# Scores of the first and last row group as three rounded products

## The chip, the cores and the metric

The kernel runs on one core of a Trainium2 chip. The metric is the device time of one execution in microseconds (us), the median of the runs. Every number of the profile comes from one profiled execution.

## What is computed

One layer of a transformer trunk: x is 2048 tokens (a grid of 32 rows by 64 columns) of 1024 features. After an RMS norm one projection gives queries, keys, values and a gate, for 16 heads of 64 features. Each token attends to the keys in a window of 8 rows by 16 columns around it, with a learned bias per offset and head. The result is gated, projected and added to x, and a last RMS norm follows.

```
h = rmsnorm(x, norm_0)
q, k, v, gate = split(h @ w_in_0, 4)
s = q . k / sqrt(64) + bias[row offset, column offset]   # in the 8 x 16 window, else -1e30
o = softmax(s) . v
x = x + (o * silu(gate)) @ w_out_0
out = rmsnorm(x, norm_f)
```

All inputs and outputs are float32.

## The kernel before

**Two kinds of matmul.** A large product of float32 data is written as three products of rounded operands: each operand t is split into h, t rounded to the type fp32r by ScalarE (ACT), and l = t - h, by VectorE (DVE), and TensorE (PE) sums h.h, h.l and l.h in one PSUM bank. Projections (L435, L559, L379 to L383) and the output product (L1346 to L1350) are of this kind. Scores (L1027) and the product of probabilities and values (L1134) are single float32 matmuls, of which each shows as two matmul records in the trace; the transposes (L1112) are float32 too, of one record each.

**Stages.** Stages one and two compute most of the projections and store queries, keys, values and gates in DRAM. From about 572 us on the main loop runs 33 cycles, m = 0 to 32. A cycle takes one pair (p, T) of `order`: two heads p and a group T of 8 grid rows. First come the eight head pairs with T = 0 (m = 0 to 7), then T = 1 and 2 in turn (m = 8 to 23), then T = 3 (m = 24 to 31). A group has keys of 11, 15, 15 and 12 grid rows (T = 0 to 3).

**A cycle.** The order of all instructions is written out by hand: what Python emits first stands first in the queue of its engine, and each engine works its queue in order. In cycle m the loop (L1429 to L1489)

- issues loads for later cycles through SyncE's queue (`begin`): keys and queries of cycle m + 1, values of m, gates of m - 1;
- feeds PE with some 16.5 matmuls of 512 columns of the remaining projections, later of the output product (`feed`; in the last group 60 and more), and calls `normalise` for the second half of cycle m - 1: a reciprocal on DVE (L1046), scalings by GpSimd (POOL, L1055) and two by ACT (L1053);
- takes a raw weight tile and splits it (`consume`: L189 on ACT, L190 on DVE), or splits rows for the output product (L1198, L1199), and runs the chain of small DVE operations for the final norm (`run_roots`: L1248 to L1255);
- transposes the probabilities of cycle m - 1 (`turns`) into six PSUM banks, which three copies on ACT and three on DVE empty (L1088);
- computes the scores of cycle m (`scores`, twice, each for two blocks of columns and two heads). A head's queries and keys lie on 64 partitions, so the two heads of a pair use the two halves of PE's rows. Every block and head takes a PSUM bank; DVE adds the bias and takes the maximum (L1035), ACT the exponential (L1041);
- multiplies the probabilities of m - 1 with the values (`values`, L1134), and DVE applies the gate (L1140).

There are eight PSUM banks, handed out as they come free. In cycle 0 there is nothing to normalise or to transpose: 8 matmuls are fed, a few more, and then come the scores.

**Buffers the change touches.** Queries and keys come as float32 into `qp` and `kp` (two buffers each), gates into `sp` (two buffers of 512 columns). `lp` (one buffer) is a landing place of the stages ahead of the loop and serves the last head pair at the end. Stages one and two use buffers of these pools, among them both of `sp`, as `slots` for split operands (L580, L805).

Of the kernel before, what the change touches and what calls it, by code (L numbers as in the profile page):

```python
# [10 lines left out]
F32 = mybir.dt.float32  # L11
F32R = mybir.dt.float32r
BF16 = mybir.dt.bfloat16
I32 = mybir.dt.int32
AF = mybir.ActivationFunctionType
OP = mybir.AluOpType
# [4 lines left out]
ROWS, GW, KH, KW = 32, 64, 8, 16  # L21
# [12 lines left out]
KEY_ROWS = [(0, 11), (4, 19), (12, 27), (20, 32)]  # L34
# [36 lines left out]
def build(ctx, tc, x, xr, xt, wg, rpb, last, w_out, n0, nf, masks, out):  # L71
    nc = tc.nc
# [8 lines left out]
    def pool(name, bufs):  # L81
        p = ctx.enter_context(tc.tile_pool(name=name, bufs=bufs))
        return lambda shape, dt, nm: p.tile(shape, dt, name=nm, tag=name)
# [3 lines left out]
    wp = pool("wp", 8)  # L87
    raw = pool("raw", 6)
    kp = pool("kp", 2)
    qp = pool("qp", 2)  # L90
    vp = pool("vp", 2)
    vhalf = []
# [4 lines left out]
            vhalf.extend((t[:, :512], t[:, 512:]))  # L97
        return vhalf.pop(0)

    sp = pool("sp", 2)  # L100
    xp = pool("xp", 8)
    mkp = pool("mkp", 1)
    pt = pool("pt", 1)
    mp = pool("mp", 10)
    ep = pool("ep", 2)

    def sixths():
        t = pt([128, 3072], F32R, "sixths")
        return [t[:, i * 512:i * 512 + 512] for i in range(6)]

    lp = pool("lp", 1)
# [5 lines left out]
    def bank(n, name):  # L117
        return banks.tile([128, n], F32, name=name, tag="bank")
# [138 lines left out]
    for n, (k, j, ph, c) in enumerate(halves):  # L257
        a = (KINDS[k] + j, ph)
# [79 lines left out]
    def must(*keys):  # L338
        assert all(k in written for k in keys), keys
        for n in range(len(later) - 1, -1, -1):  # L340
            if later[n][1] in keys:
                for _ in range(n + 1):
                    later.pop(0)[2]()
                break
# [225 lines left out]
    def stage_one():  # L570
# [6 lines left out]
        land["x12"] = [kp([128, 960], F32, "land")[:, :512] for _ in range(2)] + [xp([128, 512], F32, "land") for _ in range(2)]  # L577
        sixth = sixths()
        land["x21"] = [spot[:, k] for k in range(3)] + [lp([128, 512], F32, "land")]
        slots = [(mp, 512)] * 8 + [(sp, 512)] * 2 + sixth[:2] + [(vh, 512)] * 4  # L580
        slots += sixth[2:] + [(mp, 512)] * 2 + [(qp, 512)] * 2

        def load(f, k):
# [163 lines left out]
        for k in range(4):  # L747
            y = ev([128, 512], F32, "y")
            a, b, c = land["x11"][k], land["x12"][k], land["x22"][k]
# [48 lines left out]
    def stage_two():  # L798
        x12, x11, x21 = L2["x12"], L2["x11"], L2["x21"]
        x22 = [xp([128, 512], F32, "land") for _ in range(4)]  # L800
        sixth = sixths()
        for k in range(4):
            load_x(2, "x22", k, x22[k])
        slots = {"T2": [(mp, 512)] * 8,
                 "T3": [(sp, 512)] * 2 + sixth[:5] + [(lp, 512)],  # L805
                 "T4": [(vh, 512)] * 4 + [(mp, 512)] * 2 + [sixth[5], (qp, 512)]}

        def also(n, i):
# [120 lines left out]


    KT, VT, QT, EM, SG, E = {}, {}, {}, {}, {}, {}
    LAST, stored_at = {}, {}
    order = [(p, 0) for p in range(NP)] + [(p, T) for p in range(NP) for T in (1, 2)] + [(p, 3) for p in range(NP)]
    pairs = [(p, T, (h, h + 1)) for p, T in order for h in (0, 2)]
# [9 lines left out]
    def load_k(p, T):  # L944
        r0, r1 = KEY_ROWS[T]
        n = (r1 - r0) * GW
        must(*[("k", p, c) for c in range(r0 // 8, (r1 + 7) // 8)])

        def keys():
            t = kp([128, 960], F32, "kt")  # L950
            KT[p, T] = t.rearrange("p (r c) -> p r c", c=GW)
            nc.sync.dma_start(t[:, :n], kd[p][:, r0 * GW:r1 * GW])

        return keys

    def load_q(p, T):
        must(("q", p, T))
# [58 lines left out]
    def scores(i, between=None):  # L1016
        p, T, cs = pairs[i]
        kt, qt = KT[p, T], QT[p, T]
        r0, r1 = KEY_ROWS[T]
        got = []  # L1020
        for C in cs:
            c0, c1 = KEY_COLS[C]
            qs = slice(C * 128, C * 128 + 128)
            pst = [bank((r1 - r0) * (c1 - c0), f"s{s}") for s in range(2)]
            for s in range(2):
                a = slice(s * 64, s * 64 + 64)
                nc.tensor.matmul(pst[s], qt[a, qs], kt[a, :r1 - r0, c0:c1].rearrange("p r (s c) -> p s r c", c=8), start=True, stop=True)  # L1027
            got.append((C, pst))
        ST[i] = st = tiny.tile([128, 12], F32, name="st")
        for j, (C, pst) in enumerate(got):  # L1030
            n = (r1 - r0) * width(C)
            X[i, C] = [xp([128, 512], F32, f"x{s}")[:, :n] for s in range(2)]
            for s in range(2):
                o = 2 * j + s
                nc.vector.tensor_tensor_reduce(X[i, C][s], pst[s], EM[p, ROW_TYPE[T], COL_TYPE[C], s], -1.0, 1e38,  # L1035
                                               OP.add, OP.min, st[:, o:o + 1])
            if between and j == 0:
                between()
            for s in range(2):
                o = 2 * j + s  # L1040
                nc.scalar.activation(X[i, C][s], X[i, C][s], AF.Exp, bias=st[:, o:o + 1], scale=-1.0,  # L1041
                                     accum_out=st[:, 4 + o:5 + o])

    def normalise(i, both=False, between=None):
        st = ST.pop(i)
        nc.vector.reciprocal(st[:, 8:12], st[:, 4:8])  # L1046
        for j, C in enumerate(pairs[i][2]):
            if j and between:
                between()
            for s in range(2):  # L1050
                o = 8 + 2 * j + s
                if both and j:
                    nc.scalar.activation(X[i, C][s], X[i, C][s], AF.Copy, scale=st[:, o:o + 1])  # L1053
                else:
                    nc.gpsimd.tensor_scalar(X[i, C][s], X[i, C][s], st[:, o:o + 1], 1.0, op0=OP.mult, op1=OP.mult)  # L1055
# [305 lines left out]
    cycles = len(order)  # L1361
# [14 lines left out]
    def feed(n, calm=0):  # L1376
        credit[0] += n
        while credit[0] > 0 or credit[0] > -calm_debt and clock[0] - state["event"] < calm:
            if alive[0]:
                got = next(fill, None)  # L1380
                if got is None:
                    alive[0] = False
                    continue
            else:
                got = next(outs, None)
                if got is None:
                    due(max(credit[0], 0.0))
                    credit[0] = min(credit[0], 0.0)
                    return
            credit[0] -= got  # L1390
            due(got)
# [37 lines left out]
    for m in range(cycles + 1):  # L1429
        a = amount[m] - 8  # L1430
        begin(m)
        feed(8)
        if m:
            due_here = []
            quiet[0] = True
            if a < 12 and m > 8 and m % 2:
                normalise(2 * m - 1, True, lambda: due_here.append(split_rows() or consume(1, turn=True)))
            else:
                normalise(2 * m - 1, True)
            if a > 12:  # L1440
                run_roots()
            elif not rows_due():
                run_roots(1)
            for k in range(3):
                if m == 1 and k == 2:
                    pass
                elif a > 12 or not any(due_here) and (k < 1 or k < 2 and m > 8 and m % 2 == 0):
                    got = split_rows()
                    due_here.append(got)
                    if not got:  # L1450
                        consume(1, turn=True)
                    elif a < 12 and m % 2 == 0 and len(items) - state["used"] == 8:
                        feed(a * 0.2)
                        consume(1, turn=True)
                feed(a * 0.2)
        else:
            feed(a * 0.6)
        quiet[0] = False
        feed(a * 0.4, 8 if a > 12 else 4)
        sums = next_sums(m) == m + 1  # L1460
        if m:
            turns(m - 1)
            first_sums = m + 2 if m + 2 in pair_steps else m + 1 if sums and m + 1 not in pair_steps else None
            if first_sums:
                after = tiny.tile([128, 12], F32, name="st")
                nc.gpsimd.tensor_scalar(after[:88, 0:1], PT[m - 1][:88, 1, 0:1], ones[:88, 0:1], 1.0, op0=OP.mult, op1=OP.mult)
                tables(first_sums, 0, 1)
        if m == cycles:
            all_loads()
            feed(6)  # L1470
        else:
            scores(2 * m)
            if sums:
                tables(m + 1, 2)
            if m == 0:
                feed(first)
            scores(2 * m + 1, lambda: normalise(2 * m))
            if m == 0:
                consume(2, turn=True)
        if m:  # L1480
            values(2 * m - 2)
            values(2 * m - 1)
        runs[0] += 1
        for n in range(2, 24):
            if n < 8 and m == n - 2 or n == 8 and m == 5 or n in pair_steps and m == n - 3:
                for f in load_e(order[n][0], ROW_TYPE[order[n][1]], homes=accs if n >= 8 and n % 4 == 0 else None):
                    f()
        if m == 20:
            late_loads()  # L1489
# [52 lines left out]
```

## Time and profile before

| | us |
|---|---|
| median of 3 runs | 1057.15 |
| lowest and highest | 1056.29, 1058.18 |
| span of the profiled execution | 1054.4 |
| PE busy | 1046.1 |
| DVE busy | 696.7 |
| ACT busy | 537.2 |
| POOL busy | 252.0 |

The span goes from the first to the last instruction of one profiled execution; its own time from launch to end is not recorded apart, and the timed median lies 2.75 us above the span. In the rows of the timeline stand the start, the duration, the engine, the line of the code, the operation, what it writes and reads, shapes, the number of merged instructions, and in brackets how long the engine was idle ahead of it and who ended that. In the rows by groups stand the busy time in us and the mean of one in ns, and then the idle time ahead. In the rows by stretches stand the length, then the busy time of PE, PEld (weight loads), DVE, ACT and POOL, each with its count of instructions, the clock granted to PE as a share, the DMA engines' share and GB/s. Matmuls are pipelined: one of 512 columns lasts 0.39 us in the records, while the next starts 0.22 to 0.23 us later.

### The profile page before, as it was taken

To read this page: it belongs to the slowest core of one execution; us is meant where nothing else is said; L and a number is where in the kernel's file an instruction comes from. 1 tells how busy PE (TensorE), PEld (TensorE's weight loads), DVE (VectorE), ACT (ScalarE), POOL (GpSimd) and SP (SyncE) were. 2 spreads that over 40 slices of the span, in tenths; PEclk is the share of its full clock that TensorE was granted. 3 is DMA by queue.
4 is the path that set the end of the run, shared out by engine and by line. 5 is a ranking of instruction groups with operands and counts; after the bars stand their busy time and mean duration, and the time that the engine had idled before them with its cause. 6 is when DMAs were issued, how large, how long until landed. Compare 5 with 4: busy or idle time off the path is not lost.

```text
span 1054.4 us, 20160 instructions
## 1 busy us (share of the span) xinstructions
PE 1046.1 (99%) x7316; PEld 858.8 (81%) x7316; DVE 696.7 (66%) x1570; ACT 537.2 (51%) x1260; POOL 252.0 (24%) x342
## 2 busy tenths in 40 slices
PE   9999999999999999999999999999999999999997
PEld 7888888887888888888888788888887888888886
DVE  5476667778897625555655766687777886667554
ACT  7645223443444334232332677688787865455422
POOL 0000322312211000000002467666665322112100
PEclk9999999999999999999999999999999999999999
DMA  9634444343635433333236777778777588775352
GB/s 320 219 100 118 132 150 136 120 144 120 187 119 154 121 100 93 116 110 121 90 110 211 219 232 235 219 252 281 243 237 217 184 277 272 245 233 183 120 166 80
DMA packets 120252, 184.19 MB, mean 175 GB/s; under 512 B 10776, under 2 KB 55064, under 8 KB 120152
## 3 DMA queue, kind: packets, MB, share of 16 engines
q1 hardware_dynamic: 119720, 182.50, 55.1%
q8 instruction: 57, 0.93, 0.4%
q10 hardware_dynamic: 432, 0.40, 0.1%
q14 instruction: 43, 0.35, 0.1%
HBM read 132.53 MB, written 50.33 MB: 173 GB/s over the span
## 4 chain that ended last, share of the span: by engine, by line
PE 96%; DVE 2%; issue 1%; ACT 1%; DMA 0%; SPq 0%; DVEq 0%; ACTq 0%
PE pp L435 36%; PE pv L559 17%; PE s L1027 8%; PE o L1134 8%; PE po L1346 6%; PE po L1348 5%; PE po L1350 5%; PE ph L1112 4%; PE pp L381 2%; PE pp L383 2%; PE pp L379 2%; DVE f L418 0%; DVE x L1035 0%; DMA raw<-in_wg_dram 0%; DVE raw L424 0%
## 5 line engine op out<-in xcount | busy, mean ns | idle before, releaser
L435 PE MATMUL pp<-h,f 128*128 128x512 f32 x672 | 217.4, 389 | 0.0
L1041 ACT ACTIVATE x<-x,st 128x360 f32<-128x360 f32 (+5 forms) x256 | 151.1, 592 | 23.0 <-DVE st L1035 23.0
L1055 POOL TENSOR_SCALAR x<-x,st 128x480 f32<-128x480 f32 (+5 forms) x192 | 111.7, 599 | 153.5 <-DVE st L1046 148.6
L435 PEld LDWEIGHTS pp<-h,f 128*128 128x128 f32 x672 | 126.2, 188 | 26.2
L435 PE MATMUL pp<-t,f 128*128 128x512 f32 x558 | 141.7, 389 | 0.1
L435 PE MATMUL pp<-l,f 128*128 128x512 f32 x336 | 130.7, 389 | 0.0
L1035 DVE CUSTOM_DVE_ANT_0 x<-s,em 128x360 f32<-128x360 f32 (+5 forms) x256 | 123.0, 535 | 0.5 <-PE s L1027 0.4
L435 PEld LDWEIGHTS pp<-t,f 128*128 128x128 f32 x558 | 104.7, 188 | 22.2 <-DVE u L448 0.6
L455 POOL TENSOR_TENSOR tmp<-tmp,rb 128x512 f32<-128x512 f32 x36 | 58.4, 1622 | 268.3 <-DVE tmp L453 232.8
L995 POOL TENSOR_TENSOR em<-e,mk 128x264 f32<-128x264 f32 (+3 forms) x64 | 50.8, 825 | 259.8 <-PE pp L435 246.3
L418 DVE TENSOR_TENSOR f<-raw,f 128x512 fp32r<-128x512 f32 x105 | 76.5, 729 | 43.6 <-ACT f L417 43.5
L1346 PE MATMUL po<-woh,gh 128*128 128x512 f32 x252 | 99.8, 396 | 0.1
L1348 PE MATMUL po<-woh,gl 128*128 128x512 f32 x252 | 98.7, 391 | 0.0
L1350 PE MATMUL po<-wol,gh 128*128 128x512 f32 x252 | 98.6, 391 | 0.0
L1027 PE MATMUL s<-kt,q 64*128 64x480 f32 (+5 forms) x512 | 94.6, 487 | 0.0
L1134 PEld LDWEIGHTS o<-pta,vt 120*64 120x64 f32 (+2 forms) x1792 | 80.9, 137 | 13.9 <-DVE st L1035 13.6
L559 PE MATMUL pv<-wh,h 128*128 128x512 f32 x256 | 88.3, 390 | 0.0
L559 PE MATMUL pv<-wl,h 128*128 128x512 f32 x256 | 88.2, 390 | 0.2 <-DVE wl L542 0.2
L559 PE MATMUL pv<-wh,l 128*128 128x512 f32 x256 | 88.2, 389 | 0.0
L1088 DVE COPY pta<-ph 120x512 f32<-120x512 f32 (+5 forms) x96 | 56.9, 639 | 43.5 <-PE ph L1112 43.3
L1134 PE MATMUL o<-pta,vt 120*64 120x128 f32 (+5 forms) x1792 | 85.3, 253 | 0.0
L1027 PEld LDWEIGHTS s<-kt,q 64*128 64x128 f32 x512 | 64.9, 186 | 15.3 <-DVE pta L1088 1.3
(156 smaller groups left out, 1705.3 us busy)
## 6 DMA issues: line engine op xcount, KB each, us to landing
raw<-in_wg_dram SPq DMA_DIRECT2D x124, 256.0 KB, 4.3
row<-in_xr_dram SPq DMA_DIRECT2D x32, 256.0 KB, 4.1
vd<-v SPq DMA_DIRECT2D x32, 256.0 KB, 2.5
sgd<-sg SPq DMA_DIRECT2D x32, 256.0 KB, 2.4
q<-qd SPq DMA_DIRECT2D x32, 256.0 KB, 5.2
sgt<-sgd SPq DMA_DIRECT2D x32, 256.0 KB, 4.9
xr<-in_x_dram SPq DMA_DIRECT2D x32, 256.0 KB, 3.8
ogd<-og SPq DMA_DIRECT2D x32, 256.0 KB, 2.7
```

The lines of the kernel that those rows point to most:

```text
L418: nc.vector.tensor_tensor(t[:, 1], src, t[:, 0].bitcast(F32), OP.subtract)
L435: nc.tensor.matmul(B[n, P], t[:, int(m == 2), c], x[k][int(m == 1)], start=P in (1, 6, 5) and k == 0 and m == 0, stop=k == 3 and m == 2, s ...
L455: nc.gpsimd.tensor_tensor(tmp, tmp, rb[c], OP.mult)
L559: nc.tensor.matmul(ps[t], a[:, o], b, start=k == 0 and m == 0, stop=k == NK - 1 and m == 2)
L1027: nc.tensor.matmul(pst[s], qt[a, qs], kt[a, :r1 - r0, c0:c1].rearrange("p r (s c) -> p s r c", c=8), start=True, stop=True)
L1035: nc.vector.tensor_tensor_reduce(X[i, C][s], pst[s], EM[p, ROW_TYPE[T], COL_TYPE[C], s], -1.0, 1e38, OP.add, OP.min, st[:, o:o + 1])
L1041: nc.scalar.activation(X[i, C][s], X[i, C][s], AF.Exp, bias=st[:, o:o + 1], scale=-1.0, accum_out=st[:, 4 + o:5 + o])
L1055: nc.gpsimd.tensor_scalar(X[i, C][s], X[i, C][s], st[:, o:o + 1], 1.0, op0=OP.mult, op1=OP.mult)
L1134: nc.tensor.matmul(to.rearrange("d (h q) -> d h q", q=64) if nq > 64 else to, vt[:k, strip, s * 64:s * 64 + 64], t[:k, h, at:at + 64] if n ...
L1346: nc.tensor.matmul(p, gh, woh[q, j], start=(i == 0), stop=False)
L1348: nc.tensor.matmul(p, gl, woh[q, j], start=False, stop=False)
L1350: nc.tensor.matmul(p, gh, wol[q, j], start=False, stop=(i == NK - 1))
```

## The change

For T = 0 and T = 3 the scores become three products of rounded operands like the projections. A new function `split_kq` rounds keys and queries on ACT into `kh` (a new pool `khp` of one buffer of 768 columns) and `qh` (in `lp`), and lets DVE subtract in place, so that the loaded tiles hold the remainders. It is called in each cycle whose pair is of group 0 or 3, right behind `normalise`; in cycle 0 behind the first eight fed matmuls. `sp` has one buffer instead of two, and a buffer of `khp` takes the place of its second one in the slots of stages one and two. In these cycles a block and head has three score matmuls instead of one, with the two heads in turn.

```
+    khp = pool("khp", 1)
-    sp = pool("sp", 2)
+    sp = pool("sp", 1)
...
-        slots = [(mp, 512)] * 8 + [(sp, 512)] * 2 + sixth[:2] + [(vh, 512)] * 4
+        slots = [(mp, 512)] * 8 + [(sp, 512), (khp, 768)] + sixth[:2] + [(vh, 512)] * 4
...
-                 "T3": [(sp, 512)] * 2 + sixth[:5] + [(lp, 512)],
+                 "T3": [(sp, 512), (khp, 768)] + sixth[:5] + [(lp, 512)],
...
+    KH, QH = {}, {}
+    SPLIT = (0, 3)
...
+    def split_kq(p, T):
+        n = (KEY_ROWS[T][1] - KEY_ROWS[T][0]) * GW
+        kt, qt = KT[p, T].rearrange("p r c -> p (r c)"), QT[p, T]
+        kh, qh = khp([128, 768], F32R, "kh"), lp([128, 512], F32R, "qh")
+        nc.scalar.activation(kh[:, :n], kt[:, :n], AF.Copy)
+        nc.vector.tensor_tensor(kt[:, :n].bitcast(F32R), kt[:, :n], kh[:, :n].bitcast(F32), OP.subtract)
+        nc.scalar.activation(qh, qt, AF.Copy)
+        nc.vector.tensor_tensor(qt.bitcast(F32R), qt, qh.bitcast(F32), OP.subtract)
+        KH[p, T], QH[p, T] = kh.rearrange("p (r c) -> p r c", c=GW), qh
...
-            for s in range(2):
-                a = slice(s * 64, s * 64 + 64)
-                nc.tensor.matmul(pst[s], qt[a, qs], kt[a, :r1 - r0, c0:c1].rearrange("p r (s c) -> p s r c", c=8), start=True, stop=True)
+            terms = [(qt, kt)]
+            if T in SPLIT:
+                qh, kh, ql, kl = QH[p, T], KH[p, T], qt.bitcast(F32R), kt.bitcast(F32R)
+                terms = [(qh, kh), (qh, kl), (ql, kh)]
+            for n, (q, k) in enumerate(terms):
+                for s in range(2):
+                    a = slice(s * 64, s * 64 + 64)
+                    nc.tensor.matmul(pst[s], q[a, qs], k[a, :r1 - r0, c0:c1].rearrange("p r (s c) -> p s r c", c=8),
+                                     start=n == 0, stop=n == len(terms) - 1)
...
                 normalise(2 * m - 1, True)
+            if m < cycles and order[m][1] in SPLIT:
+                split_kq(*order[m])
             if a > 12:
                 run_roots()
...
         else:
+            split_kq(*order[0])
             feed(a * 0.6)
```

## The prediction

> **What bounds the kernel now.** I read the page first, then the waits, then stretches of the timeline engine by engine.
>
> ```profile
> PE 1046.1 (99%) x7316; PEld 858.8 (81%) x7316; DVE 696.7 (66%) x1570; ACT 537.2 (51%) x1260; POOL 252.0 (24%) x342
> ...
> PE 96%; DVE 2%; issue 1%; ACT 1%; DMA 0%; SPq 0%; DVEq 0%; ACTq 0%
> ...
> L1027 PEld LDWEIGHTS s<-kt,q 64*128 64x128 f32 x512 | 64.9, 186 | 15.3 <-DVE pta L1088 1.3
> ```
>
> TensorE (PE) is busy for 99% of the span and the chain that ended last lies on it for 96%. So a microsecond off PE is worth a microsecond, and a microsecond in which PE waits is lost for good. The third row names the wait to watch: where the scores (L1027) wait for work, it is for VectorE's (DVE's) copy of the transposes (L1088), which empties the PSUM banks that the scores fill next. Today that is 1.3 us in all.
>
> I count in cycles m of the main loop: 0 to 7 are the first row group of the eight head pairs, 24 to 31 the last. One of each, on PE:
>
> ```profile
> 619.34 1.43 PE L1112 MATMUL ph<-ident,x 64*88 64x64 f32 x44
> 620.61 2.58 PE L1027 MATMUL s<-kt,q 64*128 64x264 f32 x16
> ```
> ```profile
> 868.20 1.43 PE L1112 MATMUL ph<-ident,x 64*96 64x64 f32 x44
> 869.47 2.73 PE L1027 MATMUL s<-kt,q 64*128 64x288 f32 x16
> 872.12 2.67 PE L1134 MATMUL o<-pta,vt 96*64 96x128 f32 x56
> ```
>
> **What the change takes off PE.** A score matmul is two records (256 matmuls, x512), and a cycle's 16 records, both heads side by side, take 2.65 us in the last group (869.47 to 872.12).
>
> ```profile
> 583.67 0.39 PE L381 MATMUL pp<-l,w 128*128 128x512 f32 x1
> 583.89 0.39 PE L383 MATMUL pp<-h,w 128*128 128x512 f32 x1
> 584.21 1.31 PE L1027 MATMUL s<-kt,q 64*128 64x264 f32 x8
> 585.45 0.50 PE L379 MATMUL pp<-h,w 128*128 128x512 f32 x1
> ```
>
> A rounded product starts every 0.22 to 0.23 us at 512 columns, some 0.44 ns a column. A cycle of the last group has 288+384+384+288 = 1344 columns per head: three products are 1344 x 3 x 0.44 = 1.79 us. Some 0.3 us of the 2.65 is the change of matmul kind (584.21 follows 583.89 by 0.32 where 0.22 is usual, 585.45 comes late likewise), so 2.3 becomes 1.8 to 1.9: **0.45 us less a cycle**, likewise in the first group (1232 columns). If all sixteen cycles got it: -7.2 us. Bounds: no row shows rounded products on 64 rows. At the same price per column and two heads side by side it is 0.55; if the narrower tiles pay a fixed start, 0. Two heads one after the other are a rival.
>
> **What it adds.** Before the scores ScalarE (ACT) rounds keys and queries and DVE subtracts, each queued in order behind what was issued before. By the rows below (L189, L190: 512 columns in 0.62 and 0.69, scaled for 704 and 768 columns) the keys cost ACT 0.78 to 0.83 and DVE 0.89 to 0.96, the queries 0.62 and 0.69: 1.4 us of ACT and 1.6 of DVE a cycle. The instruction order of the changed program shows where: behind ACT's last scaling (L1053), ahead of what DVE has left in the cycle, and so ahead of its copies. The new wait on DVE is for ACT; behind it stand the weight split (L190) or the root chain (L1248), then the copies, and for these PE. In that program the scores' third and fourth column blocks take banks which the second and third copy free, and the last bank is freed by DVE's own first read of a score (L1035).
>
> *Cycle 0.* Here no transposes precede and the products follow at once.
>
> ```profile
> 584.34 0.63 ACT L517 ACTIVATE h<-raw 128x512 fp32r<-128x512 f32 x1 [1.48 <-PE pp L383]
> 584.87 0.61 ACT L359 ACTIVATE sg<-tmp 128x512 f32<-128x512 f32 x1
> 586.81 0.63 ACT L359 ACTIVATE sg<-tmp 128x512 f32<-128x512 f32 x1 [1.32 <-issue]
> ```
> ```profile
> 586.04 0.68 DVE L453 TENSOR_TENSOR tmp<-pp,u 128x512 f32<-128x512 f32 x1
> 586.64 1.52 DVE L360 SCALAR_TENSOR_TENSOR sg<-sg,tmp 128x512 f32<-128x512 f32 x2
> ```
>
> PE began these scores at 584.21. ACT is then still at gates; the last (586.81) needs the DVE result that ends at 586.72. Behind it come the rounded keys (587.4 to 588.1) and queries (to 588.7), and on DVE behind L360 (end 588.16) the remainders (589.0, 589.6). PE ends the products about 590.3 instead of 585.4: **+4.9 us**; bounds 4.3 (operations overlap at their ends) to 5.5 (each pays a full start). Keys and queries themselves were requested about 571 and are no term.
>
> *Cycles 1 to 7.*
>
> ```profile
> 616.87 0.93 ACT L1053 ACTIVATE x<-x,st 128x264 f32<-128x264 f32 x2 [0.24 <-DVE st L1046]
> 617.70 0.62 ACT L189 ACTIVATE w<-raw 128x512 fp32r<-128x512 f32 x1
> 620.08 1.54 ACT L1088 ACTIVATE pta<-ph 88x512 f32<-88x512 f32 x3 [1.77 <-PE ph L1112]
> ...
> 627.17 0.60 ACT L365 ACTIVATE k<-pp 128x512 f32<-128x512 f32 x1 [0.53 <-PE pp L383]
> ```
> ```profile
> 598.39 1.29 DVE L190 TENSOR_TENSOR w<-raw,w 128x512 fp32r<-128x512 f32 x2 [1.57 <-ACT w L189]
> 599.60 1.75 DVE L1088 COPY pta<-ph 88x512 f32<-88x512 f32 x3
> ...
> 610.10 1.75 DVE L1088 COPY pta<-ph 88x512 f32<-88x512 f32 x3 [1.56 <-PE ph L1112]
> ...
> 618.35 0.69 DVE L190 TENSOR_TENSOR w<-raw,w 128x512 fp32r<-128x512 f32 x1 [1.51 <-ACT w L189]
> 620.11 1.75 DVE L1088 COPY pta<-ph 88x512 f32<-88x512 f32 x3 [1.07 <-PE ph L1112]
> ...
> 630.35 1.75 DVE L1088 COPY pta<-ph 88x512 f32<-88x512 f32 x3 [0.53 <-PE ph L1112]
> ...
> 661.73 1.75 DVE L1088 COPY pta<-ph 88x512 f32<-88x512 f32 x3 [0.99 <-PE ph L1112]
> ```
>
> Copies end at 611.85; 5.85 later ACT is through L1053 (617.70). With the change: keys rounded 618.5, DVE subtracts to 619.3, the queries' to 619.95, L190 to 620.55; only then the copies, to 622.3. So copies to copies are 10.45 us, a ring through DVE, ACT and DVE again that no speed of PE shortens. Today the starts lie 10.01 and 10.24 apart, set by PE. From the copies of cycle 1 (599.60) to those of 7 (661.73) lie 62.1 us, six steps of 10.36; six of 10.45, two of them 0.5 longer since a projection's eviction (L365) stands ahead of L1053 and keeps it waiting, as at 627.17, make 63.7: +1.5. Cycle 1 has two weight splits (598.39) and comes 1.2 late, and 0.3 to 0.7 of shorter scores is kept at the end. Sum **+2.0 us**; bounds -1 (operations overlap) and +5 (each step pays the eviction).
>
> *Cycles 24 to 31.*
>
> ```profile
> 846.34 0.18 DVE L1046 RECIPROCAL st<-st 128x4 f32<-128x4 f32 x1 [0.40 <-ACT x L1041]
> 846.43 0.18 DVE L1248 TENSOR_SCALAR st<-st 128x1 f32<-128x1 f32 x1
> ...
> 850.49 1.75 DVE L1088 COPY pta<-ph 120x512 f32<-120x512 f32 x3
> ...
> 868.92 1.79 DVE L1088 COPY pta<-ph 96x512 f32<-96x512 f32 x3 [2.64 <-PE ph L1112]
> ...
> 887.92 1.79 DVE L1088 COPY pta<-ph 96x512 f32<-96x512 f32 x3 [4.00 <-PE ph L1112]
> ```
> ```profile
> 846.55 1.09 ACT L1053 ACTIVATE x<-x,st 128x360 f32<-128x360 f32 x2 [0.25 <-DVE st L1046]
> ```
>
> In cycle 24 DVE runs without a pause from 846.34 into the copies, and nothing covers the change: DVE waits for L1053 and the rounded keys (848.4), then subtracts to 849.9; L1248, begun at 846.43, comes 3.45 later, the copies with it. Less a little of the shorter scores: **+3.3 us** (2.5 to 4.0). In cycle 25 the same 3.5 meets a pause of 2.64 and one of about 0.4: **+0.2** (0 to 1.5). From 26 on the pauses (4.00 at 887.92, with others ahead) cover it; what is late next is the bank chain, the copies' end plus one read, 3.3 to 3.4 after the transposes begin against 3.92 today, so the 0.45 fits: six cycles, **-2.7 us** (0 to -3.2).
>
> The rest costs nothing: with one gate buffer the load waits for the product before it, which frees the buffer some 9 us ahead of need; the queue behind it (SyncE's) holds loads needed a cycle later, and the cover would be gone only if that product came that late. The landing slots move one for one.
>
> **Sum.** 4.9 + 2.0 + 3.3 + 0.2 - 2.7 = **+7.7 us**. The profiled span of 1054.4 would be 1062.1. The timed median is 1057.15, 2.75 above that span (launch and end lie outside it; the runs go from 1056.29 to 1058.18). Added there: **1064.9 us**.
>
> **Rivals.** *The clock falls in cycle 0.* PE stands nearly idle from 584.4 to 588.7.
>
> ```profile
> 1047.50:1051.40 3.90, 0.40 (x2) 0.00 (x0) 2.13 (x6) 1.92 (x6) 0.00 (x0) 1.00 0.02 4
> 1051.40:1051.80 0.40, 0.00 (x0) 0.00 (x0) 0.00 (x0) 0.00 (x0) 0.00 (x0) 1.00 0.68 256
> 1051.80:1052.20 0.40, 0.00 (x0) 0.00 (x0) 0.00 (x0) 0.00 (x0) 0.00 (x0) 0.54 1.02 394
> ```
> ```profile
> 1.19 3.24 PE L124 MATMUL zp<-z 128*128 128x512 bf16 x8 [1.19 <-DVE z L121]
> ```
>
> At the end of the kernel the granted clock (the figure before the DMA share) halves about 3.9 us after the last matmul; at the start eight matmuls take 3.24, some 0.4 each against 0.227 later. A pause of 4.3 us is just long enough. Some 3 us at half speed lose 1.4 to 1.9: +9.4, 1066.6 us. The Trainium skill ("TensorE: Matmul & The Clock Gate", Part 1) says that the clock halves after one idle window of about 3.4 us which runs freely, so that a pause must hold a whole window. By that rule the time is this rival's when the window falls well and the forecast's when not; the rows at both ends agree.
>
> *The two heads do not overlap in rounded products.* The weight loads, 0.186 each, or the unit could serialize them. Then six products a block: 1232 x 6 x 0.44 = 3.3 us and 3.5 a cycle instead of 2.2 and 2.3, over 1 us more in sixteen cycles on top of the stalls: about 1080 us. Against: today's eight records (0.4 each) fit in 1.31.
>
> *The other side: splits hidden.* If DVE and ACT let copies and scores pass on time in all cycles, cycle 0 included, the 0.45 is kept sixteen times: 1050 us. It decides at DVE's pause ahead of the copies: over about 3.5 us where roots stand there (cycles 26 on have it), over 1.6 in the first group, where 1.07 is shown. If only cycle 0 is paid: 1055.
>
> **How the numbers follow.** Forecast 0.52, clock 0.28, no overlap 0.05, only cycle 0 paid 0.07, all hidden 0.08. Range 1059 to 1072: low ends together with the most gain, high ends with the clock; the last three, 0.20, are left out. This kernel's runs tell some 0.2%, 2.1 us, from no change: faster 0.08, same 0.07, slower 0.85.
>
> **What would show it.** A hole of 4 to 5 us on PE ahead of the first scores, waiting for ACT; in cycles 1 to 7 waits of scores for L1088 and copies about 10.4 apart; a hole over 3 us in cycle 24; score stretches near 2.2 us from cycle 26 on; perhaps a clock row under 1 after the first hole. Wrong would be the sum if PE shows no hole in cycle 0, or if rounded score products start 0.2 apart instead of in pairs.

## The result, and the profile after

The changed kernel takes 1068.07 us (median of 4 runs, 1067.84 to 1068.33), the kernel before on the same chip 1057.13 (4 runs, 1056.29 to 1058.18): 10.9 us slower, ratio 1.0105 (95% interval 1.0093 to 1.0118). The forecast was 1064.9 with a range of 1059 to 1072. The direction and the range held; the forecast lies 3.2 us low, and the rival with the falling clock (1066.6) came closer.

The page of the changed kernel, engines and chain of waits:

```profile
PE 1049.7 (98%) x7444; PEld 866.5 (81%) x7444; DVE 715.9 (67%) x1602; ACT 556.6 (52%) x1292; POOL 251.9 (24%) x342
...
PE 91%; DVE 3%; ACT 2%; issue 2%; DMA 1%; SPq 0%; DVEq 0%; ACTq 0%
```

TensorE's share of the chain that ended last fell from 96% to 91%: the other five points are now work of other engines for which it waits. The groups by line name the waits; the last figures of a row are the idle time ahead of the group and what ended it:

```profile
L1045 PEld LDWEIGHTS s<-kh,qh 64*128 64x128 f32 x128 | 21.4, 194 | 14.1 <-ACT qh L965 5.0 <-DVE pta L1107 2.0 <-issue 1.9
```

The scores used to wait 1.3 us in all for DVE's copies; now 5.0 for the rounded queries (cycle 0) and 2.0 for copies. The timeline of the changed kernel around cycle 0 (start, duration, engine, line):

```profile
587.15 0.63 ACT L360 ACTIVATE sg<-tmp 128x512 f32<-128x512 f32 x1 [1.32 <-issue]
587.69 0.77 ACT L963 ACTIVATE kh<-kt 128x704 fp32r<-128x704 f32 x1
588.37 0.61 ACT L965 ACTIVATE qh<-q 128x512 fp32r<-128x512 f32 x1
...
588.49 0.89 DVE L964 TENSOR_TENSOR kt<-kt,kh 128x704 fp32r<-128x704 f32 x1
589.30 0.68 DVE L966 TENSOR_TENSOR q<-q,qh 128x512 fp32r<-128x512 f32 x1
...
589.03 0.59 PE L1045 MATMUL s<-kh,qh 64*128 64x264 f32 x2 [4.58 <-ACT qh L965]
```

The hole is there, 4.58 us, for the reason that the forecast gave: ACT's rounding stands behind the last gate. Then the same stretch by windows (PE, PEld, DVE, ACT, POOL busy with counts, granted clock, DMA share, GB/s). The clock changes at 587.58 and 594.41; the other edges are 3.41 us from these:

```profile
584.17:587.58 3.41, 0.29 (x2) 0.00 (x0) 2.65 (x5) 1.58 (x3) 0.00 (x0) 1.00 0.58 180
587.58:590.99 3.41, 1.94 (x10) 1.52 (x12) 2.46 (x5) 1.40 (x3) 0.00 (x0) 0.50 1.00 235
590.99:594.41 3.42, 3.42 (x11) 2.46 (x10) 1.56 (x8) 2.25 (x8) 1.33 (x2) 0.50 0.89 198
```

A window of 3.41 us with TensorE busy for 0.29, and the clock halves for the next two: 6.83 us at 0.50.

The ring in the first group, and cycle 24 (timeline):

```profile
617.35 0.68 DVE L966 TENSOR_TENSOR q<-q,qh 128x512 fp32r<-128x512 f32 x1
617.95 0.69 DVE L191 TENSOR_TENSOR w<-raw,w 128x512 fp32r<-128x512 f32 x1
618.56 1.75 DVE L1107 COPY pta<-ph 88x512 f32<-88x512 f32 x3
...
628.99 1.74 DVE L1107 COPY pta<-ph 88x512 f32<-88x512 f32 x3
...
858.92 0.68 DVE L966 TENSOR_TENSOR q<-q,qh 128x512 fp32r<-128x512 f32 x1
859.52 0.21 DVE L1267 TENSOR_SCALAR st<-st 128x1 f32<-128x1 f32 x1
...
863.04 1.75 DVE L1107 COPY pta<-ph 120x512 f32<-120x512 f32 x3
```

From copies to copies lie 10.43 us, and DVE goes from the subtraction through the weight split into the copies without a pause. In cycle 24 the root chain begins at 859.52, behind the subtraction, and the copies at 863.04 where they began at 850.49.

To follow single stages I compare the start of the values' first product in each cycle (L1153, before L1134), and take off the difference that already stands at 582 us, ahead of cycle 0. It arises in the start-up (up to 2.8 us, last section) and stays the same to 0.05 us from 20 us on. So cleaned, in us later than the kernel before:

| kernel | cycle 1 | cycle 8 | cycle 23 | cycle 25 | cycle 32 | timed median against before |
|---|---|---|---|---|---|---|
| changed | 8.33 | 9.46 | 9.48 | 13.27 | 12.28 | +10.9 |
| plain0 | 1.42 | 2.42 | 2.39 | 6.28 | 5.28 | +4.9 |
| warm0 | 6.26 | 7.18 | 7.12 | 10.82 | 9.66 | +10.3 |
| hh_last | 7.61 | 8.58 | 8.53 | 12.32 | 8.54 | +8.2 |
| last6 | 0.08 | 0.05 | 0.08 | 0.06 | -1.11 | -1.0 |
| early0 | 3.05 | 3.97 | 4.26 | 7.73 | 6.73 | +8.1 |
| moved | 0.48 | 0.25 | 0.21 | 1.68 | 0.36 | +0.4 |
| best | 1.96 | 1.95 | 1.93 | 1.90 | 0.82 | +0.7 |
| by_head | -0.10 | -0.12 | -0.11 | -0.11 | -1.05 | one run |
| last7 | -0.01 | -0.13 | -0.15 | -0.33 | -1.43 | -1.5 |

The profiled run before was among its fastest (span 1054.4 and the 1.8 between span and time give 1056.2, the median of that set is 1057.13), so for the changed kernel the trace shows some 1 us more than the medians. Behind cycle 32 every run gains another 0.3 us on the kernel before, whichever cycles are split; that was not followed up.

### The profile page after: what moved, and what is told of

It is laid out like the page before. It is cut to its first block, busy times and chain, and to the rows that moved or that the text cites. A ratio compares the mean times of both kernels' runs of the same rounds, so it can differ in the third digit from the quotient of the medians.

```text
span 1066.5 us, 20507 instructions
## 1 busy us (share of the span) xinstructions
PE 1049.7 (98%) x7444; PEld 866.5 (81%) x7444; DVE 715.9 (67%) x1602; ACT 556.6 (52%) x1292; POOL 251.9 (24%) x342
## 4 chain that ended last, share of the span: by engine, by line
PE 91%; DVE 3%; ACT 2%; issue 2%; DMA 1%; SPq 0%; DVEq 0%; ACTq 0%
PE pp L436 36%; PE pv L560 16%; PE s L1045 8%; PE o L1153 7%; PE po L1365 5%; PE po L1367 5%; PE po L1369 5%; PE ph L1131 3%; PE pp L382 2%; PE pp L384 2%; PE pp L380 2%; DMA kt<-kd 1%; ACT x L1060 1%; DVE f L419 0%; DVE x L1054 0%
## 5 line engine op out<-in xcount | busy, mean ns | idle before, releaser
L1153 PEld LDWEIGHTS o<-pta,vt 120*64 120x64 f32 (+2 forms) x1792 | 81.3, 138 | 11.3 <-DVE st L1054 9.8
L1153 PE MATMUL o<-pta,vt 120*64 120x128 f32 (+5 forms) x1792 | 85.7, 253 | 0.0
L418 ACT ACTIVATE f<-raw 128x512 fp32r<-128x512 f32 x105 | 63.7, 624 | 26.5 <-PE pp L436 12.5
L436 PEld LDWEIGHTS pp<-l,f 128*128 128x128 f32 x336 | 63.1, 188 | 13.2
```

The costliest lines, as they stand in the source:

```text
L418: nc.scalar.activation(t[:, 0], src, AF.Copy)
L436: nc.tensor.matmul(B[n, P], t[:, int(m == 2), c], x[k][int(m == 1)], start=P in (1, 6, 5) and k == 0 and m == 0, stop=k == 3 and m == 2, s ...
L1153: nc.tensor.matmul(to.rearrange("d (h q) -> d h q", q=64) if nq > 64 else to, vt[:k, strip, s * 64:s * 64 + 64], t[:k, h, at:at + 64] if n ...
```

## Experiments

My theory from these views: the price is one of place. Cycle 0 pays the hole and a half clock behind it, cycles 1 to 7 the ring, cycles 24 and 25 DVE without a pause; cycles 26 to 31 gain little. All kernels start from the changed one; `SPLIT` becomes a tuple of cycles where it is shown so.

### plain0: cycle 0 in float32

```
-    SPLIT = (0, 3)
+    SPLIT = (*range(1, 8), *range(24, 32))
...
-            if T in SPLIT:
+            if i // 2 in SPLIT:
...
-            if m < cycles and order[m][1] in SPLIT:
+            if m < cycles and m in SPLIT:
                 split_kq(*order[m])
...
-            split_kq(*order[0])
+            if 0 in SPLIT:
+                split_kq(*order[0])
```

> Only cycle 0 goes back to float32 products; cycles 1 to 7 and 24 to 31 stay split. Theory: in the changed kernel's trace the hole of 4.58 us ahead of the first scores (4.5 more than before) and the half clock behind it (first values start 8.5 us late, so another 3.2 to 3.6) belong to cycle 0 alone: both go, 1068.1 - 7.9 = 1060.2 us, clock 1.0 around 590 us. Rival: the late start only covered waits of cycles 1 to 7 that now show (DVE's copies would come late by themselves, as the forecast's +2.0 or its bound +5 says): 1062 to 1065 us.

Measured: 1061.4 us (1060.94 to 1062.58) against 1056.46, ratio 1.0044 (1.0029 to 1.0059). Cycle 0 alone costs 6.0 of the 10.9, and 7.0 of 12.28 by the traces. No clock falls around 590 us. The theory's 7.9 was too much: 1.4 us of lateness show in cycle 1 here too, which the theory had put down to cycle 0, so the rival had a part. The copies of cycles 2 and 3 in its timeline are as far apart as in the changed kernel, 10.41 us, and by cycle 8 it is 2.42 late: the price of cycles 1 to 7 by themselves.

```profile
611.92 1.74 DVE L1107 COPY pta<-ph 88x512 f32<-88x512 f32 x3
...
622.33 1.74 DVE L1107 COPY pta<-ph 88x512 f32<-88x512 f32 x3
```

### warm0: the hole filled

```
+            if i == 0 and C == 0:
+                for _ in range(16):
+                    nc.tensor.matmul(pst[0][:, :128], ident, ident, start=True, stop=True)
             for n, (q, k) in enumerate(terms):
```

> The changed kernel with 16 small float32 products of the identity with itself (128 columns) ahead of the first scores, in the hole, into a bank which the scores overwrite: about 3.7 us of TensorE work that delays nothing (the rounded queries arrive 4.58 us after the last product). Theory: the clock halves because TensorE idles; with the hole filled it stays at 1.0, the hole itself stays: 1068.1 less 3.2 to 3.6 = 1064.7 us, which is what was forecast. Rival: the half clock comes of something else around it (the rounded products on 64 rows themselves, or load on the other engines): clock row unchanged, 1068 us.

Measured: 1066.78 us (1065.58 to 1068.04), ratio 1.0093 (1.0077 to 1.0109). In the profiled run the clock stays at full speed, in windows like those above:

```profile
584.00:588.50 4.50, 3.81 (x34) 3.58 (x32) 3.59 (x7) 2.91 (x5) 0.00 (x0) 1.00 0.70 207
588.50:592.10 3.60, 3.26 (x19) 2.31 (x20) 2.76 (x10) 1.51 (x6) 1.36 (x2) 1.00 0.98 203
592.10:594.00 1.90, 1.90 (x10) 1.56 (x9) 0.00 (x0) 0.81 (x4) 0.00 (x0) 1.00 0.95 255
```

There the hole remains and the half clock is gone; at cycle 8 it is 7.18 late where the changed kernel is 9.46: the half clock cost 2.28 us, less than the 3.2 expected (cycle 0's scores begin 0.2 us earlier here, at 588.67 against 588.86 with the start-up taken off, so a little of it may not be the clock's). Of the four timed runs two have spans of 1063.7 and 1064.0 at a mean granted clock of 0.998, two of 1066.0 and 1066.3 at 0.995, 2.3 us more: in these the filling seems not to have been enough, though only the first has a trace. That idling lowers the clock is shown; that this filling prevents it each time is not.

### hh_last: one product instead of three in cycles 26 to 31

```
-                terms = [(qh, kh), (qh, kl), (ql, kh)]
+                terms = [(qh, kh), (qh, kl), (ql, kh)][:1 if i >= 52 else 3]
```

> In cycles 26 to 31 only the first of the three products (rounded keys by rounded queries) is made; the two with remainders are left out, all else stays (splits included). Theory A: TensorE's own steps set the 2.24 us of the scores there; with a third of the steps some 0.8 to 0.9 us are left, 1.3 to 1.4 less a cycle, about -8: 1060 us. Theory B: the chain of banks (copies on DVE, then DVE's first read of a score) sets it: the stretch stays above 2.0 us, -0.2 a cycle or less, 1067 us.

Measured: 1064.7 us (1064.46 to 1067.32), ratio 1.0079 (1.0063 to 1.0095). A cycle gains 0.63 us against float32 where three products gain 0.14 to 0.18 in the changed kernel; two thirds of the products are worth some 0.46, neither 1.3 nor 0.2. The timeline from scores to values, and the weight loads that waited:

```profile
936.59 1.43 PE L1131 MATMUL ph<-ident,x 64*96 64x64 f32 x44
...
937.83 2.10 PE L1045 MATMUL s<-kh,qh 64*128 64x288 f32 x8
939.90 0.71 PE L1153 MATMUL o<-pta,vt 96*64 96x128 f32 x10
...
938.54 0.79 PEld L1045 LDWEIGHTS s<-kh,qh 64*128 64x128 f32 x4 [0.31 <-ACT pta L1107]
939.52 0.18 PEld L1045 LDWEIGHTS s<-kh,qh 64*128 64x128 f32 x1 [0.19 <-DVE st L1054]
939.90 0.64 PEld L1153 LDWEIGHTS o<-pta,vt 96*64 96x64 f32 x12 [0.19 <-DVE st L1054]
```

Eight products take 2.07 us, because two of the loads wait for banks, one that ACT's copy empties and one that DVE's first read of a score empties; the values' own first load then waits for DVE's second read. That is the floor that the banks set: from transposes (936.59) to values (939.90) 3.31 us. Both theories fall in part: three products end above the floor (3.74, below), one would end under it.

### last6: split in cycles 26 to 31 only

```
-    SPLIT = (0, 3)
+    SPLIT = tuple(range(26, 32))
```

> Split only in cycles 26 to 31, float32 in all others. Forecast's term: 0.45 us a cycle, -2.7 against the kernel before: 1054.4 us. As the changed kernel's trace has it (0.17 a cycle): -1.0, 1056.1 us. Rival: entering the split for the first time in cycle 26 costs a hole like cycle 24's (+3.5) and nothing is left: 1058 to 1060 us.

Measured: 1055.5 us (10 runs, 1054.62 to 1057.38) against 1056.46, ratio 0.9991 (0.9981 to 1.0000): -1.0, and -1.11 by the trace, in steps of 0.16 to 0.21 a cycle. The entry in cycle 26 costs nothing. The forecast's 0.45 a cycle is not borne out.

### early0: cycle 0 split ahead of time

```
                 if i == 5:
+                    split_kq(0, 0)
                     consume(2)
...
-            split_kq(*order[0])
             feed(a * 0.6)
```

> The changed kernel with cycle 0's split issued earlier: ahead of the last weight roundings of the stage before, where ACT stood idle from about 578.4 to 582.6 us. Nothing else moves. Theory: the cost of cycle 0 is its place alone (ACT's and DVE's queues behind the last gates); the hole ahead of the first scores and the half clock behind it both go, and the changed kernel falls from 10.9 us over the kernel before to between 4.5 and 5, like the run with cycle 0 in float32 (4.9). Rival: the 1.4 us of ACT and 1.6 of DVE are missed where they now stand, and the weights that the next projection needs come late: 6 to 7 us over the kernel before.

Measured: 1065.06 us (1064.56 to 1067.77) against 1056.92, ratio 1.0083 (1.0067 to 1.0099). The theory fails here. The hole and the half clock behind it are gone in the trace (cycle 0's scores begin 0.0 late, cleaned), but the values of cycle 1 come 3.05 late, 1.6 more than in plain0. DVE's timeline shows why; its helper lines have moved by one:

```profile
583.63 1.55 DVE L965 TENSOR_TENSOR kt<-kt,kh 128x704 fp32r<-128x704 f32 x1
585.11 0.68 DVE L967 TENSOR_TENSOR q<-q,qh 128x512 fp32r<-128x512 f32 x1
...
592.40 0.43 DVE L1055 CUSTOM_DVE_ANT_0 x<-s,em 128x264 f32<-128x264 f32 x1
```

The kernel before, the same first read of a score:

```profile
588.08 0.43 DVE L1035 CUSTOM_DVE_ANT_0 x<-s,em 128x264 f32<-128x264 f32 x1
```

This run began 2.79 late; so the read comes 592.40 - 2.79 - 588.08 = 1.53 late. From its subtractions on to that read DVE pauses only where it waits for ACT (0.76 us, twice), so the 1.5 us of subtractions come out as 1.5 us of delay from this place too. The timed runs show more than the 6.7 of the trace: the profiled one holds its late start besides, and the other three have mean clocks of 0.996, 0.996 and 0.992 where the profiled one has 0.998. Where they lost it isn't recorded and stays open.

### moved: the split between the reciprocal and the scaling

```
     def normalise(i, both=False, between=None, first=None):
         st = ST.pop(i)
         nc.vector.reciprocal(st[:, 8:12], st[:, 4:8])
+        if first:
+            first()
...
-            if m < cycles and order[m][1] in SPLIT:
-                split_kq(*order[m])
```

(`first` is the split of the coming cycle; `SPLIT` and the other lines are those of plain0, so cycle 0 stays in float32.)

> Cycle 0 in float32; in cycles 1 to 7 and 24 to 31 the split is issued behind the reciprocal (L1065) and ahead of ACT's last scaling (L1072), so that DVE's subtractions don't wait for that scaling, 0.9 to 1.1 us. Beside it stands the run with cycle 0 in float32 and the split where the change puts it, 4.9 us over the kernel before. Theory (the ring of copies, exponentials, scaling, rounding, subtraction, copies sets cycles 1 to 7): the ring shrinks under the 10.0 that TensorE takes, the 2.4 us of cycles 1 to 7 go, the hole of cycles 24 and 25 shrinks from 3.9 to about 2.5; 1.0 to 1.5 us over the kernel before. Rival: the scaling is now late by 1.4 us of rounding, the transposes wait for it, and the loss stays: 4 to 5 us over.

Measured: 1057.35 us (10 runs, 1056.41 to 1060.25) against 1056.92, ratio 1.0007 (0.9997 to 1.0016), better than the 1.0 to 1.5 us that the theory left over. The loss of cycles 1 to 7 falls from 2.42 to 0.25, that of 24 and 25 from 3.9 to 1.5. Nothing but the order on ACT and DVE differs from plain0, so the ring is shown. The copies of cycles 2 and 3 (here L1109) are 10.22 us apart. That is under plain0's 10.41, though not yet the 10.01 of this step in the kernel before; over the six steps from cycle 2 to 8 the mean is 10.35 against 10.39 before:

```profile
610.86 1.75 DVE L1109 COPY pta<-ph 88x512 f32<-88x512 f32 x3
...
616.12 3.10 POOL L1076 TENSOR_SCALAR x<-x,st 128x264 f32<-128x264 f32 x6
...
618.13 1.82 DVE L964 TENSOR_TENSOR kt<-kt,kh 128x704 fp32r<-128x704 f32 x1 [0.53 <-ACT kh L963]
...
621.08 1.74 DVE L1109 COPY pta<-ph 88x512 f32<-88x512 f32 x3
```

The first group still gains nothing. DVE goes into the copies without a pause here too, and the subtraction now stands beside POOL's scaling and takes 1.82 us instead of 0.89. The Trainium skill ("GPSIMD Engine Reference", section 1) says that POOL shares its SBUF interfaces with VectorE and contends with its instructions that have two SBUF inputs; the trace agrees.

### best: both moves, cycles 24 and 25 in float32

```
+    SPLIT = (*range(8), *range(26, 32))
```

(with the edits of early0 and moved)

> Both moves together (cycle 0's split early; the others ahead of the scaling), and cycles 24 and 25 in float32, where DVE has no pause. If the costs are only where the splits stand, the sixteen cycles less two keep 0.1 to 0.2 us each: 1.0 in cycles 26 to 31 and 0 to 1.4 in cycles 0 to 7, so 1.0 to 2.4 us under the kernel before. Rival: the first group's splits cost something wherever they stand: the gain of the last six is eaten, within 1 us of the kernel before.

Measured: 1057.6 us (10 runs, 1056.52 to 1059.91) against 1056.92, ratio 1.0007 (0.9997 to 1.0017). The rival was right: the kernel is 1.96 late by cycle 1 (moved, without cycle 0's split, 0.48), cycles 2 to 8 give nothing back, and the last six gain 1.1.

### by_head: the products of one head, then those of the other

```
-            for n, (q, k) in enumerate(terms):
-                for s in range(2):
+            for s in range(2):
+                for n, (q, k) in enumerate(terms):
```

(on top of last6)

> As the run that splits in cycles 26 to 31 only, but in each column block the three products of the first head come first, then the three of the second; before, they alternated. Theory (products of the two heads, on rows 0 to 63 and 64 to 127, overlap when they stand side by side, a pair of 384 columns in 0.18 us): most pairs are broken, six products of 0.14 and 0.18 each in a block: about 3.5 to 3.9 us of scores instead of 2.24, +1.3 to +1.6 a cycle, 8 to 10 us in six. Rival (the overlap doesn't matter, banks set the pace): under 0.3 a cycle.

Measured in one run: 1054.71 us. The trace ends 1.05 us early, last6 1.11: no difference. The rival's number came true, but not for its reason. In the timeline products of the two heads alternate all the same, though the program issues three of one head and then three of the other: both heads' first products (926.19, two of them) begin ahead of either head's second (926.41), and later ones start 0.1 apart:

```profile
926.19 0.50 PE L1045 MATMUL s<-kh,qh 64*128 64x288 f32 x2
926.41 0.43 PE L1045 MATMUL s<-kt,qh 64*128 64x288 f32 x2
...
927.30 0.36 PE L1045 MATMUL s<-kh,qh 64*128 64x384 f32 x1
927.39 0.36 PE L1045 MATMUL s<-kh,q 64*128 64x384 f32 x1
927.49 0.35 PE L1045 MATMUL s<-kt,qh 64*128 64x384 f32 x1
```

The overlap between rows 0 to 63 and 64 to 127 does not need neighbours in the program: a product starts here ahead of two that stand before it. The Trainium skill ("TensorE: Matmul & The Clock Gate", Part 3) says that TensorE pulls weight loads for another row group ahead of products under way, and that the products themselves keep their order. The trace agrees with the first; the order of starts at 926.19 and 926.41 goes against the second.

### last7: split in cycles 25 to 31, ahead of the scaling

```
+    SPLIT = tuple(range(25, 32))
```

(with the edit of moved)

> Split in cycles 25 to 31 only, each time behind the reciprocal and ahead of ACT's last scaling. Theory: the split costs nothing where DVE has a pause ahead of its copies (2.64 us at cycle 25 of the kernel before) and saves 0.17 to 0.21 us a cycle of scores: seven cycles, 1.2 to 1.5 us under the kernel before (ratio 0.9986 to 0.9989), 0.2 more than the run that splits in cycles 26 to 31. Rival: cycle 25's pause does not cover it, since DVE subtracts 1.6 us and runs the roots ahead of the copies: one cycle costs 0.3 to 1.6 and the result is no better than the kernel before.

Measured: 1054.88 us (11 runs, 1053.97 to 1056.83) against 1056.39, ratio 0.9987 (0.9978 to 0.9996): 1.5 us faster than the kernel before and the fastest version here by its median (its interval and that of last6 overlap). Cycle 25 gains its 0.17 like the rest.

## Why the prediction held, and which terms were off

*Cycle 0, +4.9.* Right. warm0 without a half clock is 7.18 late at cycle 8, plain0 2.42: cycle 0 costs 4.76 by the hole alone. The order gate, keys, queries, products stands in the trace as it was worked out.

*Cycles 1 to 7, +2.0.* Right: plain0 shows 2.42, 10.41 to 10.43 from copies to copies where 10.45 was worked out, and moved takes the loss away by changing only the order. In the changed kernel 1.1 of it comes after cycle 1; the other 1.4, in cycle 1, lies within the 8.33 of the table.

*Cycle 24, +3.3, and cycle 25, +0.2.* Right in size, 3.79 together and 3.5 of it in cycle 24, but in part by luck. The root chain begins 3.44 us late (859.52 against 846.43, less the 9.65 that the run is late by then), as worked out; the copies behind it come only 2.9 late (863.04 against 850.49, less the same 9.65), where 3.45 was worked out. What fills the gap between 2.9 and 3.5 comes after the copies, where the clock is halved (last section), which the forecast did not see there.

*Cycles 26 to 31, -2.7.* This term failed: -0.99 in the changed kernel and -1.17 in last6 (from 0.06 to -1.11). The forecast took 0.44 ns a column and held that the bank chain, 3.3 to 3.4 from the transposes on, would let 0.45 through, with score stretches near 2.2. One cycle of the changed kernel:

```profile
938.55 1.43 PE L1131 MATMUL ph<-ident,x 64*96 64x64 f32 x44
939.79 0.50 PE L1045 MATMUL s<-kh,qh 64*128 64x288 f32 x2
...
941.18 0.53 PE L1045 MATMUL s<-kt,qh 64*128 64x384 f32 x2
941.37 0.53 PE L1045 MATMUL s<-kh,q 64*128 64x384 f32 x2
941.56 0.29 PE L1045 MATMUL s<-kh,qh 64*128 64x288 f32 x1
941.69 0.29 PE L1045 MATMUL s<-kt,qh 64*128 64x288 f32 x1
...
941.73 0.08 DVE L1054 DVE_READ_ACCUMULATOR2_ANT st<- 128x1 f32 x1
...
942.29 0.55 PE L1153 MATMUL o<-pta,vt 96*64 96x128 f32 x6
```

A pair of 384 columns starts every 0.19 us, one of 288 in 0.13 to 0.15: about 0.49 ns a column, so 1344 columns three times take 1.98 us and not 1.79. That is 0.19 of the missing 0.27; the rest is not split up. The whole stretch takes 2.50 (939.79 to 942.29). The chain of banks came out at the forecast's number, 3.31 in hh_last, though there over two of DVE's reads and not one. But with three products it is not what ends last: DVE's second read is done at 941.81, and the values wait behind TensorE's own products until 942.29. From the transposes that is 3.74 against 3.93 before, 0.19 less.

*The clock.* The rival came true on top of the forecast. It was given 1.4 to 1.9 us for 3 us at half speed; the trace has 6.83, and its price by warm0 is 2.28. The Trainium skill ("TensorE: Matmul & The Clock Gate", Part 1) says that the clock halves after one idle window of about 3.4 us and that the windows run freely. The records agree in the length, 3.413; that the window must be idle they do not bear out (last section). What the forecast missed is that the window after the first drop held only 1.94 us of work, and a second one at half speed followed. hh_last shows the same in cycle 0 (1.19 us of work, two windows). In the five traces with a drop in cycle 24 the window behind it held 3.38 us or more, and the clock was back after one.

*The sum.* 4.76 + 2.42 + 3.79 - 0.99 + 2.28 = 12.3, the 12.28 of the table. Against the forecast's 7.7 the clock is 2.3 and the smaller gain 1.7 of the difference, the other terms together 0.6; the medians show about 1 less, as told above. Two errors of 2.3 and 1.7 in the same direction still stayed inside the range, whose high end had been drawn for the clock. What was put at nothing was right: the table stays level from cycle 8 to 23, where the gates run through one buffer, and the stages with the moved slots add no delay behind the start-up. The other rivals fell: products of the two heads do overlap, and splits are hidden neither in all cycles nor in all but cycle 0.

## What to carry to other kernels

When a product is traded for a cheaper kind that needs its operands prepared, look first at what the preparing engines have queued ahead and behind, cycle by cycle: here the same edit costs 4.8 us in one cycle and gains 0.17 in another, and it paid only where VectorE has a pause ahead of its copies. Where a stall follows from the order on two engines in turn, issuing the preparation ahead of the step that the other engine waits for can take nearly all of it away (2.42 became 0.25). And count a hole on TensorE twice: for its length, and for the windows at half clock that it brings.

## What the runs showed of the hardware that was not expected

*The clock does not need an empty window.* In cycle 24 of the changed kernel:

```profile
857.20:860.64 3.44, 2.93 (x51) 2.29 (x49) 2.42 (x8) 1.33 (x3) 0.44 (x1) 1.00 0.88 205
860.64:864.06 3.42, 1.34 (x9) 1.10 (x11) 3.35 (x8) 2.07 (x5) 0.00 (x0) 1.00 0.91 246
864.06:867.47 3.41, 3.41 (x27) 3.13 (x27) 3.38 (x14) 2.28 (x9) 0.00 (x0) 0.50 1.03 386
```

TensorE was busy for 1.34 of 3.42 us, 39%, and the next window ran at half speed; in plain0 it was 1.75 of 3.41, 51%, with the same effect. Windows with 2.93 of 3.44, 85%, and in plain0 with 2.50 of 3.42, 73%, did not lower it (their edges are counted back from the record of the drop). What the drop in cycle 24 costs was not separated: all five kernels that were traced with the split in this place (the changed one, plain0, warm0, hh_last and early0) have it, and lose 3.5 to 3.9 us in cycles 24 and 25. In all five the copies of cycle 24 come 2.9 us late and the values 0.4 to 0.8 more; in moved, without a drop there, both come 1.7 late. So the drop is likely worth 0.4 to 0.8 us.

*The start-up decides more than some changes.* In early0 the first products of values run slowly, 0.43 us each, up to about 10.7 us:

```profile
8.33 1.05 PE L560 MATMUL pv<-wh,h 128*128 128x512 f32 x2
9.19 1.05 PE L560 MATMUL pv<-wl,h 128*128 128x512 f32 x2
...
11.65 1.07 PE L560 MATMUL pv<-wl,h 128*128 128x512 f32 x4
```

In the kernel before they are at 0.23 by 7 us:

```profile
6.38 0.63 PE L559 MATMUL pv<-wh,h 128*128 128x512 f32 x2
6.85 0.62 PE L559 MATMUL pv<-wl,h 128*128 128x512 f32 x2
```

The work there is the same in both. The clock records of the two traces reach full speed at 10.54 and 3.94 us. Profiled runs differ by up to 2.9 us (-0.11 to 2.79) before cycle 0. The two late ones, early0 and best, both have full speed only after 10 us; why is not shown, and the other runs lie within 0.6 us of each other. So a difference of spans under 3 us means little until the stages are laid beside each other.
